# Two PSUM tiles in place of one for the third and fourth quarter of the last row block

## The chip, the cores and the metric

The kernel runs on one core of one Trainium2 chip. A core has a matrix engine (TensorE, PE in the profile; PEld is its loading of weights), a vector engine (VectorE, DVE), a scalar engine (ScalarE, ACT), a general engine (GpSimd, POOL) and a queue engine (SyncE, SP). Matrix products land in PSUM, an accumulator memory of eight banks with 512 float32 numbers for each of 128 partitions; DVE and ACT read it and write it too. The metric is the device time of one execution in microseconds; the median of three runs of the kernel before is 364.58 us.

## The reference

One layer of a hybrid decoder over 256 positions of width 1024, all in float32: a projection, block attention beside a short convolution, gates, a product with `w_o`, a layer norm, a convolved feed-forward part of width 2816, and a second layer norm. What bears on the change is the end:

```python
u = causal_dwconv(x @ w_up[l], conv_w_ffn[l])
f = (jax.nn.silu(u[..., :D_FF]) * u[..., D_FF:]) @ w_down[l]
x = layer_norm(DEEPNORM_ALPHA * x + f, ln2_g[l], ln2_b[l])
```

The layer norm takes mean and variance over the 1024 columns of each row, with an epsilon of 1e-5, then a gain and a bias.

## The kernel before

The 256 positions are two row blocks of 128 (t = 0 and 1). Every float32 matrix is split into a high part that the matrix engine takes (`h`, made by ACT) and the rest (`l`, made by DVE); a product is then three products, high by high, high by low and low by high (`mm3`, lines 317 to 321; `down_on`, lines 947 to 953). The weights come in order through three buffers on the SP queue.

The order of instructions on every engine is that of the program's text; the framework adds the waits. It does so by tile: an instruction that touches a tile waits for the earlier instructions that it depends on through that tile. Engines run on their own between these waits, each through its own queue in order.

PSUM is in two pools of four banks each: `psum` hands out tiles of one bank (`acc_bank`, line 152), and `pairs` hands out tiles of two banks from two slots in turn (`ps_pair`, line 726). The FFN takes one such pair for each of its 22 parts but the first two (line 997); the last two parts, 20 and 21, have the two slots in turn, and the next call of `ps_pair` takes the slot that part 20 had.

The feed-forward part ends with 22 products of 128 rows of `w_down` each. The row block t = 0 gets all of them in turn. For t = 1 the last part is laid out so that the second norm can start on parts of the columns:

- `seed` (line 1029) writes alpha times the residual plus the sum so far into a PSUM bank, in place or into another, and for the second half also the sums over the columns. Three column ranges are seeded: `cols3`, that is 0 to 512, 512 to 768 and 768 to 1024.
- `tail_banks` (line 1038) are the three places: the bank `d10`, and the first 256 columns of each of the two banks of a pair `e`.
- Behind the residual and the statistics of t = 0 come the two seeds into `e` (line 1058), the low half of `fsr` (line 1059), which serves a product that gives the rows' mean ahead of time, and the norm of t = 0 with its two transfers out (lines 1061 to 1064).
- PE runs `down_on` for the last eight parts on `d10` (line 1068), with the two small products on `mean` (line 1071) ahead of the last part; then for the last four parts on the third quarter, and last on the fourth (lines 1072 to 1074): 12 products on each quarter.
- DVE then takes the statistics of four pieces of 256 columns each (`bn_stats`, line 1085), with the scaling of a finished range (`scaled`, line 1081) between them: two pieces of `d10`, their scaling, the third quarter, its scaling, the fourth quarter, the aggregate (line 1093). POOL raises the variance to the power -1/2 (line 1094) while DVE scales the fourth quarter (line 1095). Two passes of DVE (line 1097) finish 640 and 384 columns, and each is followed by a transfer out, on the SP and the ACT queue (line 1098).

Of the kernel before, what the change touches and what calls it, by code (L numbers as in the profile page):

```python
# [139 lines left out]
def layer_kernel(ctx: ExitStack, tc: tile.TileContext, x, wpack, cpack, ln1_g, ln1_b, ln2_g, ln2_b, out):  # L140
# [11 lines left out]
    def acc_bank(name):  # L152
        return psum.tile([P, 512], F32, tag="acc", name=name)
# [570 lines left out]
    pairs = ctx.enter_context(tc.tile_pool(name="pairs", bufs=2, space=bass.MemoryType.PSUM))  # L724

    def ps_pair(name):
        return pairs.tile([P, 2, 512], F32, tag="pair", name=name)
# [208 lines left out]
    dacc = [[acc_bank(f"d{t}{nh}") for nh in range(2)] for t in range(2)]  # L936

    def down(i, ts=(0, 1), nhs=(0, 1)):
        un = units[U[("dn", i // 2)] + i % 2]
        ft = f_tile(i)  # L940
        for t in ts:
            for nh in nhs:
                mm3(dacc[t][nh], ft[:, 0, t * P:(t + 1) * P], ft[:, 1, t * P:(t + 1) * P],
                    un["h"][:, 0, nh * 512:(nh + 1) * 512], un["l"][:, 0, nh * 512:(nh + 1) * 512],
                    i == 0, i == (NP - 1 if t == 0 else NP - LAST - 1 if nh else NP - TAIL - 1))
# [49 lines left out]
    for k, (kind, i, u) in enumerate(seq[:tail_from]):  # L995
        if kind == "g":
            pair, first_unit = ps_pair(f"pb{i}"), u
# [36 lines left out]
    seed(0, dacc[1][0], dacc[1][0], cols3[0])  # L1034
    for i in range(NP - TAIL, NP - LAST):
        down(i, (1,), (1,))
    pair = ps_pair("e")
    tail_banks = (dacc[1][0], pair[:, 0, 0:256], pair[:, 1, 0:256])

    fs = big.tile([P, LAST, 2, P], F32, tag="d8", name="fs")  # L1040
    for j in range(LAST):
# [99 lines left out]
```

## Time and profile before

| | |
|---|---|
| median of 3 runs | 364.58 us (364.22 to 365.22) |
| the profiled execution: its time | 364.13 us |
| the profiled execution: its span, first to last instruction | 362.4 us |
| granted clock of PE, mean | 0.995 |
| PE busy | 354.2 us (98%), 1935 products |
| DVE busy | 298.0 us (82%), 518 instructions |
| ACT busy | 232.5 us (64%), 415 instructions |
| bytes moved | 69.62 MB, mean 192 GB/s |

Busy times are sums over the span. An instruction's row has its start and its length in microseconds, then the engine, the line, the operation, the tiles written and read, the shape and a count where like ones are merged (the length is then that of the merged stretch); in brackets stands how long the engine was idle ahead of it and what ended that. In `128x256 f32` the first number counts partitions and the second elements on each. A tile's name is given without its number: `d` stands for `d00`, `d01`, `d10` and `d11`, and `rstats` for both row blocks' statistics.

### The profile page before, as it was taken

What the parts mean: (1) busy time and instruction counts of PE and PEld (TensorE: products, weight loads), DVE (VectorE), ACT (ScalarE), POOL (GpSimd) and SP (SyncE); (2) the same over time, 40 slices, a digit from 0 to 9 for tenths busy, and PEclk for the clock granted to TensorE, in tenths of its full rate; (3) what the DMA queues carried; (4) which work ended last, traced back from release to release, by engine and by line L of the source; (5) the groups of instructions that cost most, each with busy time, mean ns of one, the idle gap of its engine ahead of it and who ended that gap; (6) DMA issues with size and microseconds to landing.
All of it is one profiled execution on the core that took longest, in us unless ns stands there. A gap on an engine that the chain in (4) does not pass through costs nothing.

```text
span 362.4 us, 5224 instructions
## 1 busy us (share of the span) xinstructions
PE 354.2 (98%) x1935; PEld 306.0 (84%) x1935; DVE 298.0 (82%) x518; ACT 232.5 (64%) x415; POOL 21.5 (6%) x46
## 2 busy tenths in 40 slices
PE   8999999999999999999999999999999999999992
PEld 7888888898898888888888888888888888888881
DVE  4795988989886969989769888987867796999974
ACT  5675668787968957652567666664836574768800
POOL 2000000100000112310000000000000000000020
PEclk9999999999999999999999999999999999999997
DMA  7988563536563544579061754538180917663011
GB/s 291 340 306 326 185 224 125 187 128 246 208 233 117 164 185 163 219 315 332 17 233 61 288 181 169 203 145 291 66 327 14 342 60 295 233 225 123 3 58 58
DMA packets 11098, 69.62 MB, mean 192 GB/s; under 512 B 1217, under 2 KB 1473, under 8 KB 4033
## 3 DMA queue, kind: packets, MB, share of 16 engines
q1 hardware_dynamic: 10352, 67.00, 50.1%
q0 software_dynamic: 576, 2.10, 1.6%
q8 instruction: 15, 0.25, 0.3%
q10 hardware_dynamic: 144, 0.20, 0.1%
q14 instruction: 11, 0.08, 0.1%
HBM read 68.24 MB, written 1.05 MB: 191 GB/s over the span
## 4 chain that ended last, share of the span: by engine, by line
PE 59%; DVE 17%; DMA 13%; issue 6%; ACT 3%; POOLq 0%; POOL 0%; DVEq 0%; ACTq 0%
DMA raw<-in_wpack 13%; PE g L337 8%; DVE wl L209 8%; PE pb L337 5%; PE g L344 4%; PE y L337 4%; PE q L595 3%; PE k L595 3%; PE v L595 3%; PE pb L344 3%; ACT wh L199 2%; DVE fc L878 2%; PE b L337 2%; PE y L344 2%; PE c L337 2%
## 5 line engine op out<-in xcount | busy, mean ns | idle before, releaser
L209 DVE TENSOR_TENSOR wl<-raw,wh 128x1024 fp32r<-128x1024 f32 x99 | 121.9, 1234 | 24.2 <-ACT wh L199 24.0
L199 ACT ACTIVATE wh<-raw 128x1024 fp32r<-128x1024 f32 x99 | 103.7, 1053 | 27.8 <-DMA raw<-in_wpack 27.7
L337 PE MATMUL pb<-x1T,wh 128*128 128x512 f32 x320 | 76.2, 390 | 0.0
L337 PEld LDWEIGHTS pb<-x1T,wh 128*128 128x128 f32 x320 | 59.7, 188 | 12.1
L344 PEld LDWEIGHTS pb<-x1T,wl 128*128 128x128 f32 x320 | 41.0, 191 | 1.6
L344 PE MATMUL pb<-x1T,wl 128*128 128x256 f32 x320 | 41.5, 283 | 0.0
L232 DVE TENSOR_TENSOR wl<-raw,wh 128x1024 fp32r<-128x1024 f32 (+1 forms) x29 | 27.3, 982 | 6.7 <-ACT wh L231 6.4
L337 PE MATMUL g<-xT,wh 128*128 128x512 f32 x128 | 31.8, 395 | 0.0
L320 PE MATMUL d<-wl,f 128*128 128x512 f32 x76 | 29.8, 392 | 0.0
L319 PE MATMUL d<-wh,f 128*128 128x512 f32 x76 | 29.8, 392 | 0.0
L321 PE MATMUL d<-wh,f 128*128 128x512 f32 x76 | 29.7, 390 | 0.0
L231 ACT ACTIVATE wh<-raw 128x1024 fp32r<-128x1024 f32 (+1 forms) x29 | 23.7, 860 | 7.8 <-PE o L321 4.0
L337 PEld LDWEIGHTS g<-xT,wh 128*128 128x128 f32 x128 | 23.2, 188 | 4.6
L880 DVE SCALAR_TENSOR_TENSOR fc<-fb,consts,fc 128x254 f32<-128x254 f32 x40 | 19.3, 483 | 1.4
L872 ACT ACTIVATE fc<-fb,consts 128x256 f32<-128x256 f32 x40 | 18.0, 497 | 1.9 <-DVE fb L866 1.9
L878 DVE SCALAR_TENSOR_TENSOR fc<-fb,consts,fc 128x255 f32<-128x255 f32 x40 | 19.1, 479 | 0.0
L862 ACT ACTIVATE fb<-pb 128x512 f32<-128x512 f32 x20 | 11.7, 586 | 9.9 <-PE pb L344 9.9
L344 PEld LDWEIGHTS g<-xT,wl 128*128 128x128 f32 x128 | 16.4, 191 | 0.7
L321 PEld LDWEIGHTS d<-wh,f 128*128 128x128 f32 x76 | 14.3, 188 | 3.2
L344 PE MATMUL g<-xT,wl 128*128 128x256 f32 x128 | 16.6, 282 | 0.0
L320 PEld LDWEIGHTS d<-wl,f 128*128 128x128 f32 x76 | 14.3, 189 | 2.6 <-DVE wl L209 0.2
L319 PEld LDWEIGHTS d<-wh,f 128*128 128x128 f32 x76 | 14.3, 189 | 2.6
(206 smaller groups left out, 592.3 us busy)
## 6 DMA issues: line engine op xcount, KB each, us to landing
raw<-in_wpack SPq DMA_DIRECT2D x55, 1024.0 KB, 4.9
raw<-in_wpack SPq DMA_DIRECT2D x6, 896.0 KB, 5.9
xr<-in_x SPq DMA_DIRECT2D x1, 1024.0 KB, 6.9
ln<-in_ln_g POOLq DMA_DIRECT2D x2, 512.0 KB, 5.4
ln<-in_ln_b POOLq DMA_DIRECT2D x2, 512.0 KB, 6.0
raw<-in_wpack SPq DMA_DIRECT2D x2, 384.0 KB, 3.9
raw<-in_wpack SPq DMA_DIRECT2D x2, 256.0 KB, 3.7
raw<-in_wpack SPq DMA_DIRECT2D x1, 512.0 KB, 5.7
```

Source lines behind the costliest of these rows:

```text
L199: nc.scalar.activation(units[u]["h"], raw_of(u), AF.Copy)
L209: nc.vector.tensor_tensor(units[u]["l"], raw_of(u), units[u]["h"].bitcast(F32), op=ALU.subtract)
L231: nc.scalar.activation(h, src, AF.Copy)
L232: (eng or nc.vector).tensor_tensor(l, src, h.bitcast(F32), op=ALU.subtract)
L319: nc.tensor.matmul(o, ah, bh, start=start, stop=False)
L320: nc.tensor.matmul(o, ah, bl, start=False, stop=False)
L321: nc.tensor.matmul(o, al, bh, start=False, stop=stop)
L337: nc.tensor.matmul(bank, un["h"][:, k, n0:n0 + P], b[:, k].rearrange("p a s -> p (a s)"), start=k == 0, stop=False)
L344: nc.tensor.matmul(bank[:, 0:S], un["l"][:, k, n0:n0 + P], b[:, k, 0], start=False, stop=k == nk - 1)
L595: nc.tensor.matmul(banks[m][t], (xl if p == 2 else xh)[:, k, t * P:(t + 1) * P], wl if p == 1 else wh, start=k == 0 and p == 0, stop=k == ...
L878: nc.vector.scalar_tensor_tensor(c[:, 1:S], pb[:, a * S:a * S + S - 1], w_ffn(1, j), c[:, 1:S], op0=ALU.mult, op1=ALU.add)
L880: nc.vector.scalar_tensor_tensor(c[:, 2:S], pb[:, a * S:a * S + S - 2], w_ffn(0, j), c[:, 2:S], op0=ALU.mult, op1=ALU.add)
```

## The change

The places of the third and the fourth quarter are no longer the two banks of one tile. Each has a pair tile of its own, of which the first 256 columns of the first bank are used.

```diff
-    pair = ps_pair("e")
-    tail_banks = (dacc[1][0], pair[:, 0, 0:256], pair[:, 1, 0:256])
+    pairs = [ps_pair(f"e{c}") for c in range(2)]
+    tail_banks = (dacc[1][0], *(pair[:, 0, 0:256] for pair in pairs))
```

The first tile, `e0`, takes the slot that `e` had, the second, `e1`, the other slot of the pool. The lines that use `tail_banks` are unchanged, and so are the order, the number and the shapes of all instructions. The second bank of each of the two tiles is not used.

## The prediction

> **What bounds the kernel now.** The page's first part comes first, for the engine that fills the span, then the chain of waits for what sets the end, then a table of the last stretches.
>
> ```profile
> span 362.4 us, 5224 instructions
> PE 354.2 (98%) x1935; PEld 306.0 (84%) x1935; DVE 298.0 (82%) x518; ACT 232.5 (64%) x415; POOL 21.5 (6%) x46
> ```
>
> ```profile
> 346.58 0.55 POOL mv L786
> 347.13 9.66 issue
> 356.79 0.59 POOLq L1137
> ```
>
> ```profile
> 351.00:352.20 1.20, 1.20 (x8) 1.02 (x7) 0.22 (x1) 0.00 (x0) 0.00 (x0) 1.00 0.37 138
> 352.20:355.30 3.10, 3.06 (x25) 2.82 (x23) 1.98 (x7) 0.00 (x0) 0.00 (x0) 1.00 0.10 38
> 355.30:358.30 3.00, 0.00 (x0) 0.00 (x0) 2.64 (x7) 0.00 (x0) 0.55 (x1) 1.00 0.00 0
> ```
>
> PE is busy for 98% of the span, so a share of DVE's time says little; what counts is what happens after PE's last product. The chain does not help there: it books 9.66 us as "issue", that is, it found no releaser. The table does. Its columns after the length are PE, PEld, DVE, ACT and POOL, then the granted clock. PE is busy without a break until 355.30 (3.06 of 3.10 us at clock 1.00), then does nothing (0.00), while DVE works 2.64 of the next 3.00 us. So the end is PE's end plus what DVE and POOL still have to do behind it. The timeline of this tail, all engines, names that work:
>
> ```profile
> 350.19 0.75 DVE L791 SCALAR_TENSOR_TENSOR x<-x,mv,ln 128x512 f32<-128x512 f32 x1
> ...
> 351.63 0.22 DVE L1075 TENSOR_SCALAR sums<-mean,sums 128x1 f32<-128x1 f32 x1 [0.68 <-PE mean L1071]
> 352.43 0.76 DVE L1085 BATCH_NORM_STATS2 rstats<-d 128x6 f32<-128x256 f32 x2 [0.58 <-PE d L952]
> ...
> 353.72 0.75 DVE L1081 SCALAR_TENSOR_TENSOR res<-d,sums,ln 128x512 f32<-128x512 f32 x1
> 355.30 0.43 DVE L1085 BATCH_NORM_STATS2 rstats<-e 128x6 f32<-128x256 f32 x1 [0.83 <-PE e L952]
> 355.64 0.47 DVE L1081 SCALAR_TENSOR_TENSOR res<-e,sums,ln 128x256 f32<-128x256 f32 x1
> 356.03 0.42 DVE L1085 BATCH_NORM_STATS2 rstats<-e 128x6 f32<-128x256 f32 x1
> 356.48 0.26 DVE L1093 BATCH_NORM_AGGREGATE mv<-rstats 128x2 f32<-128x24 f32 x1
> ...
> 356.83 0.55 POOL L1094 TENSOR_TENSOR mv<-mv,neghalf 128x1 f32<-128x1 f32 x1 [9.70 <-DVE mv L1093]
> 357.41 1.41 DVE L1097 SCALAR_TENSOR_TENSOR res<-res,mv,ln 128x640 f32<-128x640 f32 x2 [0.33 <-POOL mv L1094]
> ...
> 358.85 0.37 ACTq L1098 DMA_DIRECT2D out<-res  x1
> ```
>
> The reader is to see the 0.83 us of idle DVE ahead of 355.30. Line 1085 there takes the statistics of the third quarter of the columns, in the first bank of tile `e`, and it was released by PE's work on `e`. Which product? PE's own timeline:
>
> ```profile
> 351.08 0.39 PE L952 MATMUL d<-wh,f 128*128 128x512 f32 x1
> 351.31 0.28 PE L1071 MATMUL mean<-ones,fsr 128*128 128x2 f32 x2
> ...
> 352.00 0.39 PE L952 MATMUL d<-wh,f 128*128 128x512 f32 x1
> 352.23 0.28 PE L952 MATMUL e<-wh,f 128*128 128x256 f32 x1
> ...
> 353.42 0.28 PE L952 MATMUL e<-wl,f 128*128 128x256 f32 x1
> 353.54 0.40 PE L952 MATMUL e<-wh,f 128*128 128x256 f32 x2
> ...
> 354.98 0.28 PE L952 MATMUL e<-wh,f 128*128 128x256 f32 x1
> ```
>
> ```profile
> L952 PE MATMUL e<-wh,f x16: 278/283/283, 352.2 to 355.0; 128*128 128x256 f32 x16
> L952 PE MATMUL e<-wl,f x8: 280/283/283, 352.3 to 354.9; 128*128 128x256 f32 x8
> L1085 DVE BATCH_NORM_STATS2 rstats<-e x2: 421/427/433, 355.3 to 356.0; 128x6 f32<-128x256 f32 x2
> ```
>
> By lines 1072 to 1074 the 24 products on `e` are 12 on the third quarter, then 12 on the fourth, each three being h, l, h. They start 0.12 us apart (24 starts, 23 steps, from 352.23 to 354.98). The fourth `l` product starts at 353.42, so the twelfth product is the first of the two at 353.54; it is done by 353.54 + 0.28 = 353.82. The last of all is done by 354.98 + 0.28 = 355.26, and DVE starts 0.04 us after that. DVE was free from 353.72 + 0.75 = 354.47, and its data had been complete for 0.65 us by then. So it waits for the whole tile and not for the bank that it reads. That DVE can be released in the middle of PE's stream is seen twice above: line 1075 starts at 351.63, 0.04 us after the pair on `mean` (351.31 + 0.28 = 351.59), and line 1085 on `d` at 352.43, 0.04 us after the end of 352.00 + 0.39, with PE running on each time.
>
> **The change part by part.** It removes no instruction, adds none and moves none. It splits one tile into two, so what changes is what each reader waits for, and where one tile lies.
>
> *The removed wait.* Line 1085 on the third quarter then waits for the product that ends at 353.82, which is past. It starts when DVE is free. How long after a 128x512 SCALAR_TENSOR_TENSOR the next one begins is seen on line 790 and 791:
>
> ```profile
> 347.89 0.75 DVE L790 SCALAR_TENSOR_TENSOR x<-x,mv,ln 128x512 f32<-128x512 f32 x1
> 348.74 0.75 DVE L791 SCALAR_TENSOR_TENSOR x<-x,mv,ln 128x512 f32<-128x512 f32 x1
> 349.41 0.75 DVE L790 SCALAR_TENSOR_TENSOR x<-x,mv,ln 128x512 f32<-128x512 f32 x1
> ```
>
> 0.85 us where it needs the result (347.89 to 348.74), 0.67 us where it doesn't (348.74 to 349.41). Here it doesn't, but both ends are kept: the start is 353.72 + 0.67 = 354.39 to 354.57. Line 1081 follows 0.34 us later (355.30 to 355.64) and line 1085 on the fourth quarter 0.39 us after that (355.64 to 356.03), so DVE could begin the fourth quarter at 355.12 to 355.30. Its data is there, by PE's last product, at 355.30 as before. **The fourth quarter is what is late next**: the stall does not go altogether, it shrinks to the 0.00 to 0.18 us ahead of 355.30. The statistics of the fourth quarter move from 356.03 to 355.30: minus 0.73 us. The gain can't exceed this, since nothing in the change lets PE end earlier.
>
> *What follows.* The aggregate of line 1093, the POOL power, the two passes of line 1097 and the two transfers of line 1098 each wait for the one ahead of them, none for a clock time of its own. They keep their distances and move by the same 0.73 us; the last issue, 358.85, becomes 358.12.
>
> *The second tile's place.* `e1` takes the other of the two slots of its pool, which the last FFN pair held. Its first write is the second seed of line 1030:
>
> ```profile
> 335.43 0.68 DVE L866 TENSOR_TENSOR fb<-pb,fb 128x512 f32<-128x512 f32 x1
> ...
> 347.27 0.43 DVE L1030 SCALAR_TENSOR_TENSOR e<-x,d 128x256 f32<-128x256 f32 x1
> 347.62 0.14 DVE L1030 DVE_READ_ACCUMULATOR e<-x,d 128x1 f32 x1
> 347.62 0.29 DVE L232 TENSOR_TENSOR fsr<-fs,fsr 128x128 fp32r<-128x128 f32 x1
> ```
>
> The last reader of that pair is line 866, done at 335.43 + 0.68 = 336.11. That is 11.16 us ahead of 347.27, so a wait for it is already met: 0, with those 11.16 us as its cover.
>
> *A wait among PE's products.* The first product on `e1`, at about 353.66, carries a dependency of its own (the seed at 347.27 and the slot), behind which eleven products queue. No row shows one in the middle of a stream of 256-wide products. From below it costs 0: the first product on `e`, at 352.23, carries the same and comes 0.23 us after 352.00, as the products around it do. From above, the row where PE's stream is interrupted for `mean`:
>
> ```profile
> L952 PE MATMUL d<-wh,f x16: 389/389/476, 346.6 to 352.0; 128*128 128x512 f32 x16
> L1085 DVE BATCH_NORM_STATS2 rstats<-d x2: 415/424/433, 352.4 to 352.8; 128x6 f32<-128x256 f32 x2
> ```
>
> The longest takes 476 ns against a median of 389, so at most 0.09 us, which would put PE's end at 355.35. I take 0, the nearer row, and keep 0.09.
>
> *Reading one bank while PE writes another.* The statistics on `d` ran while PE wrote `e` and took 415 to 433 ns; those on `e` ran with PE idle and took 421 to 433. No difference, so 0 for DVE. For PE: the ten steps from 352.23 to 353.42, most of them under DVE's reading, take 0.119 us each, and the twelve from 353.54 to 354.98 take 0.120.
>
> PE now has to signal DVE twice in this stretch and not once. The Trainium skill ("TensorE: Matmul & The Clock Gate", section "The cost: per-tile semaphore tail") puts about 26 ns on each further completion signal at the end of a set of products; by that the gain would be an estimated 0.70 us. No row here prices a signal apart.
>
> **The sum**: minus 0.73 us, with 0.64 (0.73 less 0.09) as the lower end. Span 362.4 to 361.67. The profiled execution took 364.13 us, 1.73 more than its span, and that part stays: 363.40. The median of the runs shown, 364.58, lies 0.45 above the profiled one; the forecast for it is 364.58 - 0.73 = **363.85 us**, 0.20% faster. About 0.3% (1.09 us) is what a measurement of this kernel can tell from no change, so this counts as within it.
>
> **The rivals.**
>
> *Nothing changes, 364.58.* Line 1085 might wait not for its tile but for the end of PE's whole run of products, or the two tiles might still be guarded together. For it: the wait did end with PE's last product of all, so this row alone can't tell the tile from the stream. Against it: the two releases in mid-stream, on `mean` and on `d`, each 0.04 us after that tile's last product. Both of those tiles were whole banks of their own, which is what the change makes of each quarter. A page gives this rival some weight: the Trainium skill ("Perfetto Trace Analysis", section "Matmuls") has it that groups of products in different PSUM banks let one be emptied while the next runs. The two quarters already lie in different banks, so by that alone no wait should be there to remove; the trace does not agree, with 0.83 us of idle DVE.
>
> *Slower: the second slot stalls DVE.* The place is the second seed at 347.27. If writing `e1` has to wait for something later than the last FFN pair's readers, all that DVE does behind it, the whole norm of the first row block, moves. DVE has idle time ahead of it of 0.68 us (351.63) and 0.58 us (352.43), so a stall of 1.26 us is free; the gain of 0.73 pays for more, and from 1.99 us on the kernel is slower than before. Were it held, say, until the last product ahead of the `mean` pair (351.08 + 0.39 = 351.47), the stall is 4.20 us and the loss 4.20 - 1.99 = 2.21: 366.8. Against it: what the slot held was read for the last time by 336.11, and between that pair and `e` the code takes nothing from the pool.
>
> *Half of the gain.* DVE is later at the fourth quarter than I worked out, because the third quarter's two instructions, now under PE's writing, are slower or further apart. With each of the two distances at the 0.45 us seen from 356.03 to 356.48 in place of 0.34 and 0.39, DVE comes to the fourth quarter at 354.39 + 0.90 = 355.29 to 355.47, so up to 0.17 us is lost and 0.56 gained: 364.02. The equal durations on `d` and `e` speak against more.
>
> **How the numbers follow.** The forecast gets 0.76, half of the gain 0.10, no change 0.09, the slot 0.05. The three times shown run from 0.36 below to 0.64 above their median, so a median of few runs can well move by some 0.3 us. The forecast lies 0.36 short of the bound for faster, and about three in ten of it fall beyond; with a little from the half gain that makes 0.26 for faster. The slot, and nearly nothing else, makes 0.05 for slower. The rest, 0.69, is within the bound. The range takes the forecast with its scatter and the cases of half the gain and of no change, and leaves out the slot and the outer scatter: 363.1 to 364.7.
>
> **What would show it.** In the changed kernel line 1085 on the third quarter starts at about 354.4 to 354.6, with no idle time ended by PE ahead of it; the idle time before the fourth quarter is at most 0.2 us, and that one starts 0.04 us after PE's last product; from there to the end the distances are those of before; the span is about 361.7. It would be wrong if the third quarter still began behind PE's last product (no change), if line 1030 had idle time ahead of its second seed (the slot), or if PE's last product on `e1` ended later than 355.35.

## The result and the profile after

The changed kernel takes 364.07 us (median of 22 runs, 363.61 to 364.82), the kernel before 364.96 us in the 22 runs beside them (364.22 to 366.06). The ratio is 0.9975, with a 95% interval of 0.9968 to 0.9982: 0.91 us faster, between 0.66 and 1.17. The profiled execution took 363.61 us, with a span of 361.8 us where the kernel before had 362.4.

From the page of the changed kernel, then from the table of busy times by stage (columns as before: length, PE, PEld, DVE, ACT, POOL, granted clock, share and rate of the DMA engines):

```profile
span 361.8 us, 5224 instructions
PE 354.6 (98%) x1935; PEld 306.7 (85%) x1935; DVE 298.8 (83%) x518; ACT 231.2 (64%) x415; POOL 22.0 (6%) x46
```

```profile
352.20:355.30 3.10, 3.10 (x26) 3.01 (x24) 2.61 (x8) 0.00 (x0) 0.00 (x0) 1.00 0.12 46
355.30:358.30 3.00, 0.15 (x2) 0.00 (x0) 2.53 (x6) 0.00 (x0) 0.55 (x1) 1.00 0.00 0
```

The counts of instructions are the same to the last one, 5224. DVE was busy for 1.98 us of the stretch from 352.20 to 355.30 and is now for 2.61, although this execution reaches the third quarter 0.19 us later: work has come forward to lie under PE's last products. The timeline of DVE and the queues in the changed kernel shows which:

```profile
351.82 0.22 DVE L1075 TENSOR_SCALAR sums<-mean,sums 128x1 f32<-128x1 f32 x1 [0.82 <-PE mean L1071]
352.62 0.76 DVE L1085 BATCH_NORM_STATS2 rstats<-d 128x6 f32<-128x256 f32 x2 [0.58 <-PE d L952]
...
353.91 0.75 DVE L1081 SCALAR_TENSOR_TENSOR res<-d,sums,ln 128x512 f32<-128x512 f32 x1
354.58 0.42 DVE L1085 BATCH_NORM_STATS2 rstats<-e 128x6 f32<-128x256 f32 x1
354.92 0.47 DVE L1081 SCALAR_TENSOR_TENSOR res<-e,sums,ln 128x256 f32<-128x256 f32 x1
355.49 0.43 DVE L1085 BATCH_NORM_STATS2 rstats<-e 128x6 f32<-128x256 f32 x1
355.95 0.26 DVE L1093 BATCH_NORM_AGGREGATE mv<-rstats 128x2 f32<-128x24 f32 x1
...
358.32 0.37 ACTq L1098 DMA_DIRECT2D out<-res  x1
```

And PE's timeline there, from the product ahead of the third quarter to its last:

```profile
352.19 0.39 PE L952 MATMUL d<-wh,f 128*128 128x512 f32 x1
352.42 0.28 PE L952 MATMUL e<-wh,f 128*128 128x256 f32 x1
...
353.61 0.28 PE L952 MATMUL e<-wl,f 128*128 128x256 f32 x1
353.73 0.40 PE L952 MATMUL e<-wh,f 128*128 128x256 f32 x2
353.97 0.28 PE L952 MATMUL e<-wl,f 128*128 128x256 f32 x1
...
355.17 0.28 PE L952 MATMUL e<-wh,f 128*128 128x256 f32 x1
```

The bracket with 0.83 us ahead of the third quarter is gone. Line 1085 there starts at 354.58, 0.67 us after line 1081 and while PE still writes the fourth quarter. The fourth quarter starts at 355.49, which is 0.04 us after PE's last product (355.17 + 0.28 = 355.45). It comes 0.57 us after the scaling ahead of it, where the kernel before had 0.39 (355.64 to 356.03): the 0.18 us between them is what is left of the stall. Counted in the same way, from start to start, the stall before was 0.91 us: 1.58 us from line 1081 to line 1085 (353.72 to 355.30), where 0.67 are enough. The 0.83 in the bracket counts only the time in which DVE did nothing.

The two executions reach this place at different times (PE's first product on the third quarter starts at 352.23 before and at 352.42 after; its first product of line 952, ahead of the first instruction that the change touches, already starts at 346.55 and at 346.75), so the gain is read as a distance, from that product to the issue of the last transfer:

| kernel | first product on the third piece | last issue | distance |
|---|---|---|---|
| before | 352.23 | 358.85 | 6.62 |
| changed | 352.42 | 358.32 | 5.90 |

That is 0.72 us less. It lies within the interval of 0.66 to 1.17; the rest of the 0.91 us is not told from scatter.

### The profile page after: what moved, and what is told of

It reads as the page before. It is cut to its first block, busy times and chain, and to the rows that moved or that the text cites. A ratio compares the mean times of both kernels' runs of the same rounds, so it can differ in the third digit from the quotient of the medians.

```text
span 361.8 us, 5224 instructions
## 1 busy us (share of the span) xinstructions
PE 354.6 (98%) x1935; PEld 306.7 (85%) x1935; DVE 298.8 (83%) x518; ACT 231.2 (64%) x415; POOL 22.0 (6%) x46
## 4 chain that ended last, share of the span: by engine, by line
PE 95%; issue 3%; DVE 1%; POOLq 0%; POOL 0%; DVEq 0%
PE pb L337 20%; PE pb L344 11%; PE g L337 8%; PE d L319 5%; PE d L320 4%; PE d L321 4%; PE g L344 4%; PE y L337 4%; PE q L595 3%; PE v L595 3%; PE k L595 3%; PE b L337 2%; PE y L344 2%; PE c L337 2%; PE o L320 2%
```

## The experiments

All seven compute the whole layer. The line numbers in their rows can be off by one against the code printed above, where an edit adds a line or takes one out.

**The change once more**, run beside the next three; no edit.

> The changed kernel once more, as the measure for the next three. Tile theory (a reader waits for all products on its tile): 0.7 to 0.9 us below the kernel before, ratio about 0.998; the statistics of the third quarter start with no idle time ended by PE, those of the fourth 0.04 us after PE's last product. Rival, chance placement of the runs: no difference from the kernel before.

364.13 us against 364.86, ratio 0.9978 (0.9965 to 0.9991). In its timeline the first product on the third quarter starts at 352.48 and the last issue is at 358.38: 5.90 again. The third quarter's statistics start with no idle time ahead of them:

```profile
353.96 0.75 DVE L1081 SCALAR_TENSOR_TENSOR res<-d,sums,ln 128x512 f32<-128x512 f32 x1
354.63 0.42 DVE L1085 BATCH_NORM_STATS2 rstats<-e 128x6 f32<-128x256 f32 x1
```

So the difference is not the luck of the first runs.

**Two tiles, in other banks.** Each quarter has a tile of one bank from the other pool, and the small product on `mean` moves from that pool into a pair.

```diff
-    pair = ps_pair("e")
-    tail_banks = (dacc[1][0], pair[:, 0, 0:256], pair[:, 1, 0:256])
+    tail_banks = (dacc[1][0], *(acc_bank(f"e{c}")[:, 0:256] for c in range(2)))
...
-    mean = acc_bank("mean")
+    mean = ps_pair("mean")[:, 0]
```

> Two tiles as in the change, but each a one-bank tile of the other pool, in the banks that the first row block's sums held, and the small product on mean in a pair. Tile theory: where the tiles lie does not matter, so the same as the changed kernel, 0.7 to 0.9 us below the kernel before, third quarter released early. Rival, the place (the other slot or bank makes DVE or PE faster): the gain goes, ratio 1.000.

364.24 us against 364.86, ratio 0.9975 (0.9964 to 0.9987): the gain of the change, at another place. Its timeline, with the first product on the third quarter and the last issue, 5.91 us apart:

```profile
353.16 0.28 PE L952 MATMUL e<-wh,f 128*128 128x256 f32 x1
```

```profile
354.65 0.75 DVE L1080 SCALAR_TENSOR_TENSOR res<-d,sums,ln 128x512 f32<-128x512 f32 x1
355.32 0.42 DVE L1084 BATCH_NORM_STATS2 rstats<-e 128x6 f32<-128x256 f32 x1
```

```profile
359.07 0.37 ACTq L1097 DMA_DIRECT2D out<-res  x1
```

Which of these banks the two tiles have made no difference.

**One tile, in another bank.** Both quarters are halves of one bank of the other pool.

```diff
-    pair = ps_pair("e")
-    tail_banks = (dacc[1][0], pair[:, 0, 0:256], pair[:, 1, 0:256])
+    both = acc_bank("e")
+    tail_banks = (dacc[1][0], both[:, 0:256], both[:, 256:512])
```

> One tile for both quarters as before, but one bank of the other pool, its two halves. Tile theory: as the kernel before (ratio 1.000 within 0.1%), 0.8 us of DVE idle ahead of the third quarter, ended by PE's last product. Rival, the place: anything that differs from the kernel before by half a microsecond.

364.83 us against 364.86, ratio 0.9995 (0.9983 to 1.0007). The stall is back at its old size. PE's last product starts at 355.92 and ends 0.04 us ahead of the statistics of the third quarter:

```profile
355.92 0.28 PE L952 MATMUL e<-wh,f 128*128 128x256 f32 x1
```

```profile
356.24 0.43 DVE L1085 BATCH_NORM_STATS2 rstats<-e 128x6 f32<-128x256 f32 x1 [0.83 <-PE e L952]
```

From the first product on the third quarter to the last issue it is 6.62 us (353.17 to 359.79), as in the kernel before. Two banks of one tile (the kernel before) and one bank (this one) wait alike, and two tiles in either pool don't. It is the tile that is guarded, and its place has no share in the gain.

**As many tiles, tied elsewhere.** The first half and the third quarter are the two banks of one tile; the fourth quarter has its own.

```diff
-    seed(0, dacc[1][0], dacc[1][0], cols3[0])
+    pairs = [ps_pair(f"e{c}") for c in range(2)]
+    seed(0, pairs[0][:, 0], dacc[1][0], cols3[0])
...
-    pair = ps_pair("e")
-    tail_banks = (dacc[1][0], pair[:, 0, 0:256], pair[:, 1, 0:256])
+    tail_banks = (pairs[0][:, 0], pairs[0][:, 1, 0:256], pairs[1][:, 0, 0:256])
```

> Same number of tiles as the change, tied differently: the first two quarters and the third are the two banks of one tile, the fourth has its own. Tile theory: the statistics of the first half now wait for the third quarter's products and start 1.43 us later against PE's stream; the chain of DVE from there (2.69 us from the first statistics to the fourth quarter's when nothing else holds it) puts the fourth quarter at 0.52 us later than in the kernel before, so about 0.5 us slower than it and 1.25 us slower than the change. Rival, DVE waits for the end of PE's whole stream or two tiles as such are what helps: as the kernel before, or 0.7 us faster.

366.25 us against 364.86, ratio 1.0033 (1.0022 to 1.0043): slower by 1.20 us (0.80 to 1.57), where 0.5 was expected. The direction is the tile theory's and against both others, the size is not. DVE's timeline has the part that was expected, a long wait ahead of the first half's statistics, and behind it 2.68 us to the fourth quarter's (355.40 to 358.08; expected 2.69):

```profile
355.40 0.76 DVE L1085 BATCH_NORM_STATS2 rstats<-e 128x6 f32<-128x256 f32 x2 [2.01 <-PE e L952]
...
358.08 0.42 DVE L1085 BATCH_NORM_STATS2 rstats<-e 128x6 f32<-128x256 f32 x1
```

What was missed is on PE. Its timeline, where the first half's last eight parts begin, and DVE's seed of the third quarter:

```profile
346.95 0.39 PE L321 MATMUL d<-wh,f 128*128 128x512 f32 x1
347.92 0.50 PE L952 MATMUL e<-wh,f 128*128 128x512 f32 x1 [0.58 <-DVE e L1030]
```

```profile
347.38 0.43 DVE L1030 SCALAR_TENSOR_TENSOR e<-x,d 128x256 f32<-128x256 f32 x1 [0.23 <-PE d L321]
```

The writer is guarded by tile as well. The first product on the first half waits for DVE's seed of the third quarter (347.38 + 0.43 = 347.81), in the other bank of the same tile: 0.97 us from 346.95 to 347.92. With no wait at this place it is 0.23, as the free one of the next two runs shows, so 0.74 us are added to all that follows. Behind it PE is slower for a while: from that product to PE's last it takes 8.60 us (347.92 to 356.52), 0.17 more than the 8.43 of the kernel before (346.55 to 354.98). From the end of PE's last product to the fourth quarter's statistics it is 1.28 us (356.80 to 358.08) where the kernel before has 0.77 (355.26 to 356.03), so the readers' part is 0.51, as expected. The three make 1.42 us, inside the interval.

**The writer's wait alone, and the same without it.** Both runs move the sum of the first half into the first bank of a pair and write one more seed of 256 columns that nobody reads. In the first run it goes into the second bank of that pair, in the second into a pair of its own.

```diff
-    seed(0, dacc[1][0], dacc[1][0], cols3[0])
+    half = ps_pair("h")
+    seed(0, half[:, 0], dacc[1][0], cols3[0])
...
-    pairs = [ps_pair(f"e{c}") for c in range(2)]
-    tail_banks = (dacc[1][0], *(pair[:, 0, 0:256] for pair in pairs))
+    tail_banks = (half[:, 0], *(acc_bank(f"e{c}")[:, 0:256] for c in range(2)))
...
+    seed(0, half[:, 1, 0:256], dacc[1][1][:, 0:256], cols3[1])
     for c in (1, 2):
```

The second run differs from the first in two lines:

```diff
-    half = ps_pair("h")
+    half, spare = ps_pair("h"), ps_pair("spare")
...
-    seed(0, half[:, 1, 0:256], dacc[1][1][:, 0:256], cols3[1])
+    seed(0, spare[:, 0, 0:256], dacc[1][1][:, 0:256], cols3[1])
```

> The writer's wait alone: the third and fourth quarters have a tile each, as in the change; the sum of the first half moves into the first bank of a pair, and one more seed of 256 columns is written into that pair's second bank, which nobody reads. Tile theory: no reader waits longer than in the change, but PE's first product on the first half waits for the further seed in the other bank, as in the run with the tiles tied elsewhere: about 0.7 us of delay for that product, 0.7 to 0.9 us for the end, which eats the change's gain: ratio 0.999 to 1.000. Rival (the slowness of the run with the tiles tied elsewhere was the readers' wait alone): as the change, ratio 0.9975.

> As the run before with the further seed written into a tile of its own. It has the same instructions. Tile theory: PE's first product on the first half follows the one ahead of it after 0.23 us again, the further 0.34 us of DVE go into its idle time, and the time is the change's, ratio about 0.9975. Rival (it is DVE's further instruction that costs): as the run before.

Tied: 364.56 us against 364.60, ratio 1.0004 (0.9993 to 1.0014). Free: 363.99 against the same 364.60, ratio 0.9985 (0.9974 to 0.9995). The timelines at the place, tied and then free:

```profile
346.93 0.39 PE L321 MATMUL d<-wh,f 128*128 128x512 f32 x1
347.36 0.43 DVE L1030 SCALAR_TENSOR_TENSOR h<-x,d 128x256 f32<-128x256 f32 x1 [0.23 <-PE d L321]
...
347.84 0.50 PE L952 MATMUL h<-wh,f 128*128 128x512 f32 x1 [0.52 <-DVE h L1030]
...
348.18 0.39 PE L952 MATMUL h<-wl,f 128*128 128x512 f32 x1
...
359.57 0.37 ACTq L1099 DMA_DIRECT2D out<-res  x1
```

```profile
346.87 0.39 PE L321 MATMUL d<-wh,f 128*128 128x512 f32 x1
347.10 0.39 PE L952 MATMUL h<-wh,f 128*128 128x512 f32 x1
...
358.68 0.37 ACTq L1099 DMA_DIRECT2D out<-res  x1
```

Tied, PE's next product comes after 0.91 us (346.93 to 347.84), free after 0.23 (346.87 to 347.10): 0.68 us. To the last issue it is 12.64 us against 11.81, so 0.83 us for a wait on a bank that the product doesn't touch. Most of the other 0.15 is again PE's slower stream behind the wait, from its first product on the first half to its last of all: 8.58 us tied (347.84 to 356.42), 8.42 free (347.10 to 355.52). The two intervals of the ratios overlap by a little, so the size is read from these traces and not from the times. The further seed itself costs nothing that can be told: the free run has the change's ratio within the intervals, and from the same product on its 11.81 us are the changed kernel's 11.80 (346.52 to 358.32).

**A smaller last piece.** The change with the second half split 320 and 192.

```diff
-    cols3 = (slice(0, 512), slice(512, 768), slice(768, D))
+    cols3 = (slice(0, 512), slice(512, 832), slice(832, D))
...
-    tail_banks = (dacc[1][0], *(pair[:, 0, 0:256] for pair in pairs))
+    tail_banks = (dacc[1][0], *(pair[:, 0, 0:n] for pair, n in zip(pairs, (320, 192))))
...
-        seed(c, tail_banks[c], dacc[1][1][:, 256 * c - 256:256 * c], cols3[c])
+        seed(c, tail_banks[c], dacc[1][1][:, cols3[c].start - 512:cols3[c].stop - 512], cols3[c])
```

> The change with the second half split 320 and 192 and not 256 and 256. Theory (PE's last product is what ends last now, DVE waits 0.18 us for it ahead of the fourth piece): 64 columns more cost DVE about 2 x 0.067 us ahead of PE's end, which fits into the 0.18, and 64 fewer save 0.067 us behind it, so from PE's last product to the last issue 2.80 us and not 2.87, as long as PE's stream is no longer than before (2.98 us from the first product on the third piece to the last one's end 3.03 at most). Time 0.8 to 0.9 us below the kernel before, not to be told from the change. Rival (DVE is the bound already): the fourth piece starts 0.1 us or more after PE's end, and nothing is gained.

364.37 us against 364.82, ratio 0.9982 (0.9968 to 0.9995). Against the kernel before it gains; that it is a little behind the change lies within the intervals, but the timeline says why it would be:

```profile
353.02 0.31 PE L952 MATMUL e<-wh,f 128*128 128x320 f32 x1
...
355.20 0.27 PE L952 MATMUL e<-wl,f 128*128 128x192 f32 x1
355.31 0.39 PE L952 MATMUL e<-wh,f 128*128 128x192 f32 x2
355.54 0.27 PE L952 MATMUL e<-wl,f 128*128 128x192 f32 x1
...
355.99 0.28 PE L952 MATMUL e<-wh,f 128*128 128x192 f32 x1
356.30 0.36 DVE L1085 BATCH_NORM_STATS2 rstats<-e 128x6 f32<-128x192 f32 x1 [0.18 <-PE e L952]
...
359.07 0.37 ACTq L1098 DMA_DIRECT2D out<-res  x1
```

The part behind PE's end is as expected: from 355.99 + 0.28 = 356.27 to 359.07 are 2.80 us, where the change has 358.32 - 355.45 = 2.87. And the last piece again starts 0.03 us after PE's last product, so PE is what it waits for. But the condition of the expectation fails: PE needs 356.27 - 353.02 = 3.25 us for the two pieces, not the change's 355.45 - 352.42 = 3.03. Three products of 192 columns take 0.34 us (355.20 to 355.54), 0.113 each, and three of 256 took 0.36 (353.61 to 353.97). Fewer columns hardly made them faster. The distance of the table comes to 6.05 us, 0.15 more than in the change.

## Why the prediction was right

**The bound** held. The stall ahead of the third quarter was a wait for the whole tile. The runs with two tiles and with one tile elsewhere tell this from the place of the tiles: 5.91 us from the first product to the last issue with two, 0.83 us of idle DVE with one.

**The removed wait**: the third quarter was to start 0.67 to 0.85 us after the scaling of the first half; it started 0.67 after. What was to be left of the stall was 0.00 to 0.18 us; it is 0.18. The fourth quarter starts 0.04 us after PE's last product, as the limit of the gain had it.

**The sum**: minus 0.73 us was forecast, and the distances within the traces show minus 0.72. The medians show minus 0.89, the ratio minus 0.66 to 1.17, which holds it. That 364.07 lies above the forecast of 363.85 comes from its base: the median of three runs of the kernel before was 364.58, that of 22 is 364.96. Less 0.73 that is 364.23. The prediction took 0.3% as the least that can be told from no change; with 22 runs of each kernel 0.25% was told, in an interval from 0.18% to 0.32%.

**What follows** kept its distances: 2.82 us from the fourth quarter's statistics to the last issue before (356.03 to 358.85), 2.83 after (355.49 to 358.32).

**The second slot** costs nothing: the second seed has no idle time ahead of it, as this row of the changed kernel's timeline shows, and the two tiles of the other pool give the same time.

```profile
346.95 0.43 DVE L1030 SCALAR_TENSOR_TENSOR e<-x,d 128x256 f32<-128x256 f32 x1 [0.23 <-PE d L321]
...
347.29 0.47 DVE L1030 SCALAR_TENSOR_TENSOR e<-x,d 128x256 f32<-128x256 f32 x1
```

**The wait among PE's products** costs nothing that shows: from the fourth `l` product on the third quarter to the first on the fourth quarter are 0.36 us for three products (353.61 to 353.97), as elsewhere, and the whole stream of 24 starts takes 2.75 us in both kernels (352.23 to 354.98, 352.42 to 355.17). The Trainium skill ("TensorE: Matmul & The Clock Gate", section "The cost: per-tile semaphore tail") has its 26 ns for each completion signal behind a set of small products that share the array, which these are not. Neither the starts here nor the 0.04 us from PE's last product to DVE, the same before and after, shows such a cost.

**Not foreseen** was one wait more that the change removes, listed as unchanged work: the two seeds wrote one tile, and the second waited for the first. They were 0.52 us apart (346.75, in the row of the kernel before that follows, to 347.27) and are 0.34 apart now. It gains nothing, because DVE waits for PE ahead of line 1075 all the same, now for longer: its idle time there was 0.68 us before and is 0.82 after.

```profile
346.75 0.43 DVE L1030 SCALAR_TENSOR_TENSOR e<-x,d 128x256 f32<-128x256 f32 x1 [0.25 <-PE d L321]
```

**Two readings were weaker than they looked.** The comparison of PE's steps under DVE's reading (0.119 us) with later ones (0.120) does not set reading against no reading: line 1081 reads `d` from 353.72 to 354.47, in the middle of the later ones. The changed kernel is the better row: with the third quarter read beside the last products, PE's stream takes the same 2.75 us. And the slot's price took none of the slack that the prediction itself left ahead of the fourth quarter: with up to 0.18 us there, the kernel would be slower only from a stall of 1.99 to 2.17 us on.

Of the rivals, "nothing changes" falls with the runs of one and of two tiles; the stall at the slot did not come; and the half gain did not, since DVE's instructions on the third quarter took as long under PE's writing (0.42 and 0.47 us) as with PE idle (0.43 and 0.47).

## What to carry to other kernels

Where a reader is released by the last of several groups of products and not by its own, look at whether the groups share a tile: here a tile was guarded as a whole, for its readers and its writers, although its banks were separate. The gain is at most the idle time that the wait made, less what then waits for the same end, so work out the next wait before counting it. A bank lent to another group of the same tile can cost as much on the writer's side (0.83 us here) as on the reader's. Giving a smaller piece to the end helps only as long as the products on it get shorter in proportion.

## What the runs showed of the hardware beside this

Fewer columns in a product can save less than their share of the time. The steps between products, each with new weights, were 0.23 us at 512 columns (346.87 to 347.10), 0.12 at 256 and 0.113 at 192: a half of the columns is worth a half of the time, but the next quarter off is worth almost nothing. Why was not tried.

Where PE had waited 0.52 us for DVE, the first product behind the gap took 0.50 us and the next came 0.34 us after it (347.84 to 348.18), where 0.39 and 0.23 are the rule. The run with the tiles tied elsewhere has the same behind its wait of 0.58 us: 0.50 and 0.34 (347.92 to 348.26). In its table of busy times, for the gap and for the stretch behind it, the granted clock is 1.00 in both, so the granted clock does not show what it is, and that was not tried.

```profile
347.30:347.90 0.60, 0.04 (x1) 0.00 (x0) 0.52 (x3) 0.00 (x0) 0.48 (x1) 1.00 0.00 0
347.90:349.00 1.10, 1.08 (x5) 0.89 (x6) 1.10 (x5) 0.00 (x0) 0.00 (x0) 1.00 0.00 0
```
